# Four split-weight buffers, Fourier tiles by outputs, early swaps of q, and a softmax scaled by GpSimd, in a two-layer encoder

## The chip, the cores and the metric

The kernel runs on one core of a Trainium2 chip. The metric is the device time of one execution in microseconds, the median of several runs. The core has five engines that work side by side, each through its own queue in order: TensorE (PE in the profile; PEld is its weight load), VectorE (DVE), ScalarE (ACT), GpSimd (POOL) and SyncE (SP), which here issues most of the transfers.

## The reference

Two layers of a bidirectional encoder over 272 positions (16 learned meta tokens and 256 tokens), width 2048, in float32:

```python
for i in range(DEPTH):
    h = _rmsnorm(h_stream, norm_mix[i])
    proj = h @ w_in[i]                                  # q | k | v | f | ga | gf
    q = _rope_2d(_rmsnorm(q, q_norm[i]), cos_r, sin_r, cos_c, sin_c)
    k = _rope_2d(_rmsnorm(k, k_norm[i]), cos_r, sin_r, cos_c, sin_c)
    ...
    p = jax.nn.softmax(s, axis=-1)                      # 8 heads on 2 kv heads, head 128
    a_br = attn @ w_attn_br[i]
    fr = jnp.fft.fft2(fg, axes=(1, 3), norm="ortho").real
    s_br = fr.reshape(B, L, FOURIER_WIDTH) @ w_four[i]
    merged = g_attn * a_br + g_four * s_br              # sigmoid gates
    h_stream = h_stream + merged @ w_out[i]
    h2 = _rmsnorm(h_stream, norm_ffn[i])
    up = h2 @ w_up[i]                                   # gate | value, 2 x 5632
    u_gate = _dwconv3_centred(up[..., :D_FF], w_conv[i], b_conv[i])
    h_stream = h_stream + (jax.nn.silu(u_gate) * u_val) @ w_down[i]
return h_stream[:, N_META:]
```

## The kernel before

Activations are kept transposed, channels on the 128 partitions and positions along the free dimension. Each float32 product is made of three matmuls on a type with a shorter mantissa: a high and a low part of the weights (wh, wl) and of the activations (H, L), high times high, high times low and low times high (lines 372 to 374).

All weights run through one stream of 948 chunks of 512 KB, in the order of `order` (lines 191 to 225), with the products of layer 1's last matrices mixed in. A chunk is [128, 4, 256]: four slices of the contracted dimension by 256 outputs. `load_raw` (257) fetches a chunk on SP's queue into one of `RAW = 7` buffers `raw` (in the last feed-forward, every third chunk into one of two buffers `raw5`). `split_w` (294) rounds it on ACT into wh (300) and takes the remainder on DVE into wl (303); `wp` gives wh and wl three buffers each. `advance` (269) loads ahead and puts the splits up to `LOOK = 2` chunks ahead into the list `todo`; `pump` emits them, one after every sixth matmul of a `group` (346). In layer 0 the Fourier weights are folded first: `fold_w` (288) adds and subtracts the halves of a chunk on DVE into the single buffer `wpm` (291), which is then split in place of the raw chunk.

Besides the weight stream, generators in `shadow` are advanced one at a time by `step`, also after every sixth matmul: statistics, rotary work, attention, transposes. `push(gen, wait)` adds one. The order of instructions on each engine is set by a planner that takes the program's order as priority and the costs of a model; inside `manual_schedule` (lines 741, 1168, 1170) and `keep_in_program_order` the order written is the order issued.

The branches of a layer follow `BRANCH_ORDER`. `four_group` (388) multiplies the Fourier branch by its weights, from two chunks. Each of these chunks holds, for two of the four blocks of the contracted dimension and both signs e, all 256 outputs. The loop makes the first 128 outputs (m = 0) from chunk 0 and then chunk 1, and then the other 128 (m = 1) from both again; so both are split (`pump(i0 + 1)`, 395) before it begins. In layer 1 these weights, and those of the Fourier input, have been folded into DRAM beforehand (`prefold`), and the Fourier input is one long product `folded_f` (805) of 16 chunks, placed between the second and the third group of q, with ACT and DVE ordered by hand (1168 to 1172).

For q, `head_evac` (902) brings a group out of PSUM, and a generator `q_stage` (1011) does the rest: `swap` (921) exchanges halves of 64 and 32 channels by four transfers on SP's queue, then the statistics, then `rope` (927) on DVE. The tiles of `head_evac`, `swap`, the gates and the folds share one ring `r` of seven buffers.

`attention` works on 18 items per layer (two kv heads; the meta queries and 4 heads x 2 blocks). For an item, `scores` makes the product, its maximum and the exponentials with their sum (ACT, into the tile pe, 1078); `normalise` (1081) takes the reciprocal of the sum on DVE and writes pe times it into one of three tiles pn, as 256 columns (1086) and three copies of the 16 meta columns (1087); `transposed` (1091), an item later, transposes pn on PE and splits it into PH and PL; `values` multiplies by V.

GpSimd does little: powers for the norms (`pow_half`, 513), and between the branches and the last feed-forward `weight_sums` (553): a tiny copy `tick` that waits for the latest wl, then a DRAM transfer, over and over.

Of the kernel before, what the change touches and what calls it, by code (L numbers as in the profile page):

```python
# [10 lines left out]
F32 = mybir.dt.float32  # L11
# [167 lines left out]
def encoder_kernel(ctx, tc, xT, params, consts, bmat, cfold, csign, w_fl, w_f64c, w_in, w_abr, w_four, w_f64, w_out, w_up, w_down, w_vn, w_dn, w_dt, out):  # L179
# [72 lines left out]
            chunks.append(ch)  # L252
    st = {"raw": 0, "fetch": 0, "next": 0, "grp": 0}
    raws, splits = {}, {}
    RAW, LOOK = 7, 2

    def load_raw(i):
        src, n = chunks[i]
# [22 lines left out]
    def pump(upto=None):  # L281
        if upto is None:
            if todo:
                todo.pop(0)[1]()
        while upto is not None and todo and todo[0][0] <= upto:
            todo.pop(0)[1]()

    def fold_w(i):
# [2 lines left out]
            tc.keep_in_program_order(nc.vector.tensor_tensor(r[:, o:o + 2], raws[i][:, 0:2], raws[i][:, 2:4], op=op))  # L291
        raws[i] = r

    def split_w(i, a, b, parts="hl"):
        if i not in splits:
            splits[i] = tuple(wp.tile([P, CW, MG * P], F32R, tag=t, name=f"{t}{i}") for t in ("wh", "wl"))
        h, lo = splits[i]
        r = raws[i]
        if "h" in parts:
            nc.scalar.copy(h[:, a:b], r[:, a:b])  # L300
        st["wl"] = lo
        if "l" in parts:
            nc.vector.tensor_tensor(lo[:, a:b], r[:, a:b], h[:, a:b].bitcast(F32), op=ALU.subtract)  # L303
            if b == CW:
                del raws[i]
# [82 lines left out]
    def four_group(key, fr, x64, w64, evac):  # L388
        k, chs = order[st["grp"]]
        assert k == key, (k, key)  # L390
        st["grp"] += 1
        i0 = st["next"]
        st["next"] += len(chs)
        advance(i0 + 1 + LOOK)
        pump(i0 + 1)
        ws = [splits.pop(i0 + j) for j in range(2)]
        for m in range(MG):
            sl = slice(m * P, (m + 1) * P)
            ps = [psum.tile([P, 512], F32, tag="mm", name=f"ps_s{m}{e}") for e in range(2)]
            for j in range(2):  # L400
                h, lo = ws[j]
                for c in range(2):
                    kt = 2 * j + c
                    for e in range(2):
                        x = al(fr[:, kt, e])
                        o2 = st2(ps[e][:, :2 * TH].rearrange("p (r n) -> p r n", r=2))
                        nc.tensor.matmul(o2, h[:, 2 * e + c, sl], x, start=kt == 0, stop=False)
                        nc.tensor.matmul(st2(ps[e][:, :TH]), lo[:, 2 * e + c, sl], x[:, 0], start=False, stop=e == 1 and kt == 3)
                    step()
                    pump()  # L410
                if m == 1 and j == 0:
                    advance(i0 + 2 + LOOK)
            nc.tensor.matmul(st2(ps[0][:, :TH]), w64[:, sl], al(x64), start=False, stop=True)
            evac(m, ps)
# [194 lines left out]
    for l in range(DEPTH):  # L609
# [6 lines left out]
        with tc.tile_pool(name=f"mix{l}", bufs=1) as mp:  # L616
# [391 lines left out]
            for pn in pns:  # L1008
                nc.gpsimd.memset(pn[:, 0:P], 0.0)

            def q_stage(i, qp, qsq):
                kv, j = i // 2, i % 2
                sl = slice(2 * j, 2 * j + 2)
                if j == 0:
                    qvs.append(small.tile([P, 9], F32, tag="qv", name="qv"))
                    qsms.append(small.tile([P, 2, 4, NM], F32, tag="sqm", name="sqm", bufs=2))
                qv, qsm = qvs[kv], qsms[kv]
                qs = swap(qp)
                yield 3
                nc.vector.tensor_copy(qsm[:, :, 2 * j:2 * j + 2, :], qsq[:, :, 0:NM].unsqueeze(1).to_broadcast([P, 2, 2, NM]))  # L1020
                d4 = qv[:, 4 * j:4 * j + 4]
# [25 lines left out]
            def attention(kv, rq):  # L1047
# [11 lines left out]
                def scores(item):  # L1059
# [13 lines left out]
                    nc.vector.tensor_reduce(mx, ss[:, :T], axis=AX.X, op=ALU.max)  # L1073
                    nb = small.tile([P, 1], F32, tag="nb", name="nb")
                    nc.vector.tensor_scalar(nb, mx, rcol, -1.0, op0=ALU.mult, op1=ALU.mult)
                    pe = mp.tile([P, T], F32, tag="pe", name="pe", bufs=2)
                    sm = small.tile([P, 1], F32, tag="sm", name="sm")
                    nc.scalar.activation(hv(pe), de(ss[:, :T]), AF.Exp, bias=nb, scale=rcol, accum_out=sm)
                    return pe, sm

                def normalise(pe, sm):
                    rs = small.tile([P, 1], F32, tag="rs", name="rs")
                    nc.vector.reciprocal(rs, sm)
                    pn = pns[cnt[0] % 3]
                    cnt[0] += 1
                    nc.vector.tensor_scalar(pn[:, P:3 * P], pe[:, NM:T], rs, None, op0=ALU.mult)
                    nc.vector.tensor_scalar(pn[:, 0:96].rearrange("p (a b) -> p a b", b=32)[:, :, 0:NM], _rep(pe[:, 0:NM], 3),
                                            rs, None, op0=ALU.mult)
                    return pn

                def transposed(item, pn):
# [59 lines left out]
            for i in range(4):  # L1151
                if not (last and i == 1):
                    ps = group((l, "q", i), xr(lo), W)
                    qq = head_evac(ps, prm[:, P_QN + l:P_QN + l + 1], "qp", lo)
                if last:
                    if i in (0, 2):
                        until(hold, "vt" if i == 0 else "fold")
# [8 lines left out]
                if last and i == 1:  # L1166
                    until(hold, "ahead")
                    with tc.manual_schedule(engines={mybir.EngineType.DVE}):
                        ps = group((l, "q", i), xr(lo), W)
                        with tc.manual_schedule(engines={mybir.EngineType.Activation}):  # L1170
                            qq = head_evac(ps, prm[:, P_QN + l:P_QN + l + 1], "qp", lo)
                            folded_f(slots, E)
                    o1_tiles()
                    push(folded_chan(E), 1)
# [335 lines left out]
def _four(w):  # L1510
# [6 lines left out]
    w64 = np.zeros((d, 64, D), w.dtype)  # L1517
    w64[:, 0:8] = w64[:, 32:40] = w[:, [P * (2 * i + m) + HC for m in range(2) for i in range(4)]]
    w64 = np.ascontiguousarray(w64.reshape(d, 64, NG, MG * P).transpose(0, 2, 1, 3))
    return _tiles(wz[:, rows]), w64  # L1520


def _fl(w):
# [47 lines left out]
```

## Time and profile before

| | |
|---|---|
| median of 3 runs | 2402.76 us (2401.09 to 2405.47) |
| profiled execution | 2399.24 us, of which span 2397.2 us |
| granted TensorE clock | 0.998 |
| DMA, mean | 276 GB/s |

The span is the time from the first to the last instruction; the profiled execution's own time stands beside it. Busy times count an engine's instructions, without waits. In the rows of waits, the engine and line that waited come first, then what ended the wait, then the total, the number and the longest. In a timeline row come start, duration, engine, line, operation, tiles, and in brackets the idle time before it and what ended it.

### The profile page before, as it was taken

The numbers are of one execution on the slowest core, as the hardware profiler recorded it, in microseconds if no ns is written. First come the engines' busy times: TensorE is split into PE (matmuls) and PEld (weight loads), VectorE is DVE, ScalarE is ACT, GpSimd is POOL, SyncE is SP. The second block draws the span as 40 slices with busy tenths as digits, with TensorE's granted clock in tenths as the row PEclk, the third lists the DMA queues.
The fourth block names the chain that finished last, engine by engine and source line by source line (L and its number), as shares of the span: only waits on it lengthen the run. The fifth ranks groups of instructions, "written<-read, shape, count | busy, mean of one in ns | idle before, by whom it ended". The sixth has DMA issues, their size and how long they took to land.

```text
span 2397.2 us, 47622 instructions
## 1 busy us (share of the span) xinstructions
PE 2367.0 (99%) x18992; PEld 2305.8 (96%) x18992; DVE 1819.8 (76%) x2889; ACT 1307.1 (55%) x1893; POOL 133.4 (6%) x265
## 2 busy tenths in 40 slices
PE   9999999999999999999999999999999999999999
PEld 8999999999999999999998999999989999999988
DVE  7787867877767556777568887776878889888798
ACT  6555534554444334444455555445676666666565
POOL 0000100100000000000000000000000000000000
PEclk9999999999999999999999999999999999999999
DMA  7556999989999999999875646888889988988887
GB/s 278 173 159 216 289 295 304 297 278 346 313 303 327 315 330 314 316 327 308 264 256 181 190 150 216 264 291 247 290 294 301 323 291 301 305 304 279 260 279 251
DMA packets 171215, 660.69 MB, mean 276 GB/s; under 512 B 19424, under 2 KB 24672, under 8 KB 170096
## 3 DMA queue, kind: packets, MB, share of 16 engines
q1 hardware_dynamic: 152528, 538.07, 64.0%
q0 software_dynamic: 17024, 117.45, 19.4%
q8 instruction: 149, 2.44, 0.4%
q10 hardware_dynamic: 1440, 2.13, 0.3%
q14 instruction: 74, 0.61, 0.1%
HBM read 635.91 MB, written 136.31 MB: 322 GB/s over the span
## 4 chain that ended last, share of the span: by engine, by line
PE 81%; DVE 6%; ACT 2%; DMA 1%; issue 1%; SPq 0%; POOL 0%; ACTq 0%; DVEq 0%; POOLq 0%
PE ps_p L1415 9%; PE ps_ug L374 6%; PE ps_ug L373 6%; PE ps_ug L372 6%; PE ps_uv L368 4%; PE ps_d L374 3%; PE ps_uv L373 3%; PE ps_uv L372 3%; PE ps_d L373 3%; PE ps_uv L374 3%; PE ps_d L372 3%; DVE wl L303 3%; PE ps_o L372 2%; PE ps_o L373 2%; PE ps_o L374 2%; PE ps_uv L369 2%
## 5 line engine op out<-in xcount | busy, mean ns | idle before, releaser
L303 DVE TENSOR_TENSOR wl<-raw,wh 128x1024 fp32r<-128x1024 f32 (+1 forms) x937 | 1127.6, 1217 | 469.8 <-ACT wh L300 458.4
L300 ACT CAST wh<-raw 128x1024 fp32r<-128x1024 f32 (+1 forms) x937 | 964.6, 1040 | 752.1 <-PE ps_ug L373 197.2
L374 PE MATMUL ps_ug<-xHL,wl 128*128 128x272 f32 (+1 forms) x1408 | 390.6, 277 | 0.8 <-DVE wl L303 0.6
L372 PE MATMUL ps_ug<-xHL,wh 128*128 128x272 f32 (+1 forms) x1408 | 390.7, 278 | 0.0
L373 PE MATMUL ps_ug<-xHL,wh 128*128 128x272 f32 (+1 forms) x1408 | 390.0, 277 | 0.0
L373 PEld LDWEIGHTS ps_ug<-xHL,wh 128*128 128x128 f32 x1408 | 267.4, 190 | 2.1
L372 PEld LDWEIGHTS ps_ug<-xHL,wh 128*128 128x128 f32 x1408 | 267.4, 190 | 2.1
L374 PEld LDWEIGHTS ps_ug<-xHL,wl 128*128 128x128 f32 x1408 | 267.5, 190 | 1.6 <-DVE wl L303 1.5
L372 PE MATMUL ps_uv<-xHL,wh 128*128 128x272 f32 x704 | 196.4, 279 | 0.0
L373 PE MATMUL ps_uv<-xHL,wh 128*128 128x272 f32 x704 | 196.4, 279 | 0.0
L374 PE MATMUL ps_uv<-xHL,wl 128*128 128x272 f32 x704 | 196.4, 279 | 0.0
L372 PE MATMUL ps_d<-gHL,wh 128*128 128x272 f32 x704 | 196.4, 279 | 0.0
L373 PE MATMUL ps_d<-gHL,wh 128*128 128x272 f32 x704 | 196.4, 279 | 0.0
L374 PE MATMUL ps_d<-gHL,wl 128*128 128x272 f32 x704 | 196.4, 279 | 0.0
L1415 PE MATMUL ps_p<-wh,opnd 128*128 128x512 f32 x688 | 177.5, 380 | 0.5 <-ACT wh L300 0.5
L368 PE MATMUL ps_uv<-xHL,wh 128*128 128x512 f32 x448 | 150.8, 383 | 0.1
L372 PE MATMUL ps_ga<-xHL,wh 128*128 128x272 f32 (+1 forms) x512 | 144.0, 281 | 0.0
L372 PE MATMUL ps_gf<-xHL,wh 128*128 128x272 f32 (+1 forms) x512 | 143.0, 279 | 0.0
L374 PE MATMUL ps_gf<-xHL,wl 128*128 128x272 f32 (+1 forms) x512 | 141.8, 277 | 0.0
L373 PE MATMUL ps_ga<-xHL,wh 128*128 128x272 f32 (+1 forms) x512 | 141.8, 277 | 0.0
L374 PE MATMUL ps_ga<-xHL,wl 128*128 128x272 f32 (+1 forms) x512 | 141.8, 277 | 0.0
L373 PE MATMUL ps_gf<-xHL,wh 128*128 128x272 f32 (+1 forms) x512 | 141.8, 277 | 0.0
(372 smaller groups left out, 5840.8 us busy)
## 6 DMA issues: line engine op xcount, KB each, us to landing
raw<-in_w_up SPq DMA_DIRECT2D x320, 512.0 KB, 5.6
raw<-in_w_in SPq DMA_DIRECT2D x191, 512.0 KB, 4.5
raw<-in_w_down SPq DMA_DIRECT2D x88, 512.0 KB, 6.8
raw<-ft SPq DMA_DIRECT2D x80, 512.0 KB, 4.8
raw<-in_w_out SPq DMA_DIRECT2D x64, 512.0 KB, 6.5
ft<-in_w_dn POOLq DMA_DIRECT2D x30, 1024.0 KB, 12.1
raw<-in_w_dn SPq DMA_DIRECT2D x60, 512.0 KB, 5.0
raw<-in_w_abr SPq DMA_DIRECT2D x32, 512.0 KB, 5.6
```

Of the source, the lines that this page charges most:

```text
L300: nc.scalar.copy(h[:, a:b], r[:, a:b])
L303: nc.vector.tensor_tensor(lo[:, a:b], r[:, a:b], h[:, a:b].bitcast(F32), op=ALU.subtract)
L368: nc.tensor.matmul(o2, h[:, c, sl], ab, start=kt == 0, stop=False)
L369: nc.tensor.matmul(o, lo[:, c, sl], ab[:, 0], start=False, stop=kt == nk - 1)
L372: nc.tensor.matmul(o, h[:, c, sl], a, start=kt == 0, stop=False)
L373: nc.tensor.matmul(o, h[:, c, sl], b, start=False, stop=False)
L374: nc.tensor.matmul(o, lo[:, c, sl], a, start=False, stop=kt == nk - 1)
L1415: nc.tensor.matmul(st2(ps[h]), x, al(w[:, 512 * h:512 * h + 512]), start=fresh and (s_, q) in BEGIN and first, stop=(s_, q) in END and end ...
```

## The change

Four edits:

1. `RAW, LOOK = 5, 3`: five raw buffers, splits up to three chunks ahead, and (`split_tiles`) four buffers each for wh and wl. The bytes are the same, 13 tiles before and after.
2. The host lays the Fourier weights out by outputs: a chunk holds both signs and all four blocks of the contracted dimension for 128 outputs. `four_group` then needs chunk m for the outputs m, asks for chunk 0 alone before it starts and for chunk 1 when it comes to m = 1, and calls the second `advance` after the first half instead of after three quarters. The matmuls, their order and widths stay.
3. `swap` is called at once after `head_evac` and its tile handed to `q_stage`, instead of at the first step of `q_stage`; for the second q of layer 1 this is before `folded_f`.
4. In the softmax, the exponentials go straight into the tile pn (the tile pe is gone), the three copies of the meta columns are made by ACT from unscaled values, and GpSimd multiplies the whole tile of 384 columns by the reciprocal in place; DVE keeps the reciprocal.

```diff
-    RAW, LOOK = 7, 2
+    RAW, LOOK = 5, 3
...
+    def split_tiles(i):
+        return tuple(wp.tile([P, CW, MG * P], F32R, tag=t, name=f"{t}{i}", bufs=LOOK + 1) for t in ("wh", "wl"))
+
     def split_w(i, a, b, parts="hl"):
         if i not in splits:
-            splits[i] = tuple(wp.tile([P, CW, MG * P], F32R, tag=t, name=f"{t}{i}") for t in ("wh", "wl"))
+            splits[i] = split_tiles(i)
...
         advance(i0 + 1 + LOOK)
-        pump(i0 + 1)
-        ws = [splits.pop(i0 + j) for j in range(2)]
         for m in range(MG):
             sl = slice(m * P, (m + 1) * P)
             ps = [psum.tile([P, 512], F32, tag="mm", name=f"ps_s{m}{e}") for e in range(2)]
+            pump(i0 + m)
+            h, lo = (w.rearrange("p c n -> p (c n)").rearrange("p (e k n) -> p e k n", e=2, k=4) for w in splits.pop(i0 + m))
             for j in range(2):
-                h, lo = ws[j]
...
-                        nc.tensor.matmul(o2, h[:, 2 * e + c, sl], x, start=kt == 0, stop=False)
-                        nc.tensor.matmul(st2(ps[e][:, :TH]), lo[:, 2 * e + c, sl], x[:, 0], start=False, stop=e == 1 and kt == 3)
+                        nc.tensor.matmul(o2, h[:, e, kt], x, start=kt == 0, stop=False)
+                        nc.tensor.matmul(st2(ps[e][:, :TH]), lo[:, e, kt], x[:, 0], start=False, stop=e == 1 and kt == 3)
                     step()
                     pump()
-                if m == 1 and j == 0:
+                if m == 0 and j == 1:
                     advance(i0 + 2 + LOOK)
...
-            def q_stage(i, qp, qsq):
+            def q_stage(i, qp, qsq, qs):
...
-                qs = swap(qp)
                 yield 3
...
-                    pe = mp.tile([P, T], F32, tag="pe", name="pe", bufs=2)
+                    pn = pns[cnt[0] % 3]
+                    cnt[0] += 1
                     sm = small.tile([P, 1], F32, tag="sm", name="sm")
-                    nc.scalar.activation(hv(pe), de(ss[:, :T]), AF.Exp, bias=nb, scale=rcol, accum_out=sm)
-                    return pe, sm
-
-                def normalise(pe, sm):
+                    nc.scalar.activation(hv(pn[:, P - NM:3 * P]), de(ss[:, :T]), AF.Exp, bias=nb, scale=rcol, accum_out=sm)
+                    nc.scalar.copy(pn[:, 0:96].rearrange("p (a b) -> p a b", b=32)[:, :, 0:NM], _rep(pn[:, P - NM:P], 3))
+                    return pn, sm
+
+                def normalise(pn, sm):
                     rs = small.tile([P, 1], F32, tag="rs", name="rs")
                     nc.vector.reciprocal(rs, sm)
-                    pn = pns[cnt[0] % 3]
-                    cnt[0] += 1
-                    nc.vector.tensor_scalar(pn[:, P:3 * P], pe[:, NM:T], rs, None, op0=ALU.mult)
-                    nc.vector.tensor_scalar(pn[:, 0:96].rearrange("p (a b) -> p a b", b=32)[:, :, 0:NM], _rep(pe[:, 0:NM], 3),
-                                            rs, None, op0=ALU.mult)
+                    nc.gpsimd.tensor_scalar(pn, pn, rs, None, op0=ALU.mult)
                     return pn
...
                     qq = head_evac(ps, prm[:, P_QN + l:P_QN + l + 1], "qp", lo)
+                    qq += (swap(qq[0]),)
...
                             qq = head_evac(ps, prm[:, P_QN + l:P_QN + l + 1], "qp", lo)
+                            qq += (swap(qq[0]),)
                             folded_f(slots, E)
...
-    return _tiles(wz[:, rows]), w64
+    t = _tiles(wz[:, rows]).reshape(d, NG, 2, P, 2, 2, MG, P).transpose(0, 1, 6, 3, 4, 2, 5, 7)
+    return np.ascontiguousarray(t).reshape(d, NG, MG, P, CW, MG * P), w64
```

## The prediction

> **What bounds the kernel now.** The page comes first: the span and the busy times of the engines.
>
> ```profile
> span 2397.2 us, 47622 instructions
> PE 2367.0 (99%) x18992; PEld 2305.8 (96%) x18992; DVE 1819.8 (76%) x2889; ACT 1307.1 (55%) x1893; POOL 133.4 (6%) x265
> ```
>
> TensorE (PE) is busy for 2367.0 of 2397.2 us. The change adds and removes no matmul, so it can only win part of the 30 us in which PE stands still, and a little more where a stall has side effects. The table of busy time by stage tells where those 30 us lie (PE busy is the first engine column, the granted clock stands before the last two).
>
> ```profile
> 120.00:225.00 105.00, 101.24 (x867) 100.14 (x867) 86.97 (x206) 56.66 (x116) 4.29 (x5) 1.00 0.52 172
> 225.00:475.00 250.00, 244.80 (x2091) 242.57 (x2091) 188.54 (x301) 120.50 (x175) 26.47 (x50) 1.00 0.94 297
> 475.00:1243.00 768.00, 768.00 (x6630) 767.92 (x6630) 521.32 (x776) 363.12 (x467) 51.61 (x111) 1.00 0.94 310
> 1243.00:1335.00 92.00, 87.05 (x731) 85.33 (x729) 77.19 (x139) 53.85 (x91) 4.08 (x12) 0.96 0.63 202
> 1335.00:1455.00 120.00, 115.37 (x994) 112.36 (x994) 96.63 (x237) 66.98 (x142) 3.84 (x4) 1.00 0.47 147
> ```
>
> The 768 us of layer 0's feed-forward have no gap, and one matmul there takes 768.0 / 6630 = 0.116 us, so a chunk of 24 matmuls takes 2.8 us. The gaps lie in layer 0's attention (120 to 225), its branches (225 to 475), the folded Fourier product of layer 1 (1243 to 1335) and layer 1's attention (1335 to 1455). Next, PE's waits by cause (total us, times, longest).
>
> ```profile
> PE ps_s L408 <- DVE wl L303: 4.3, 8, 0.7
> PE ps_f L847 <- DVE wl L303: 3.9, 1, 3.9
> PE ps_pt L1095 <- DVE pn L1086: 2.9, 4, 1.3
> PE ps_pv L1119 <- DVE PL L1109: 2.2, 4, 1.2
> PE ps_s L407 <- ACT wh L300: 2.0, 5, 1.1
> PE ps_uv L369 <- DVE wl L303: 1.1, 3, 0.6
> ```
>
> Four of the six rows wait for the split of a weight chunk (wh, wl; `ps_uv` in the last feed-forward), two for the softmax. The change touches both.
>
> **The Fourier branch, `four_group`.** The first group of layer 0 in the order of time, PE and VectorE (DVE):
>
> ```profile
> 222.32 1.28 DVE L291 TENSOR_TENSOR wpm<-raw 128x512 f32<-128x512 f32 x2
> 223.48 0.22 PE L408 MATMUL ps_s<-fr,wl 128*128 128x138 f32 x1
> 224.77 1.23 DVE L303 TENSOR_TENSOR wl<-wpm,wh 128x1024 fp32r<-128x1024 f32 x1 [0.47 <-ACT wh L300]
> 224.79 0.62 PE L407 MATMUL ps_s<-fr,wh 128*128 128x276 f32 x3 [1.09 <-ACT wh L300]
> ```
>
> The group stopped at 223.5, after the eight matmuls (some 0.9 us) of its first chunk: both chunks are needed in turn for the first half of the outputs, and the second was still being folded (L291), rounded (L300) and split (L303). From 223.48 to 224.79 is 1.31 us; 138 columns take 0.06 (half of the 0.116 of 272), so 1.25 are lost, of which the row shows 1.09, since a modelled matmul is longer than its slot. So each of the 13 stalls (8 on L408, 5 on L407) costs some 0.14 more than its row: 4.3 + 2.0 + 13 x 0.14 = 8.1 us. With the tiles by outputs, the second chunk is due only after 16 matmuls and the short one of L413, at about 224.7, and with a fourth split buffer its fold can begin a chunk (2.8 us) earlier. The fold's own buffer stays single, so one chunk's chain, 3.7 us from 222.32 to the end of wl at 226.0, follows the one before it. Even so wl, ready at 226.0, comes 2.8 earlier by 223.2 and is due at 224.7. I take -7.8 (0.3 left); the ends are -3 (fold order unchanged, only the 1.1 us of later need won in each of 8 groups, less than the whole stall) and -8.1. Matmuls, their widths and the bytes are the same, so the new layout itself costs nothing.
>
> **The folded product of layer 1, with the early swap.** Here is the one long stop, on PE, the DMA queue of SyncE (SP) and DVE.
>
> ```profile
> 1292.69 0.33 PE L843 MATMUL ps_f<-hA,wh 128*128 128x276 f32 x1
> 1292.92 0.33 PE L843 MATMUL ps_f<-hA,wh 128*128 128x276 f32 x1
> 1297.73 0.48 PE L847 MATMUL ps_f<-hA,wl 128*128 128x138 f32 x1 [3.89 <-DVE wl L303]
> 1298.45 0.54 PE L843 MATMUL ps_f<-hA,wh 128*128 128x276 f32 x1
> 1298.89 0.53 PE L843 MATMUL ps_f<-hA,wh 128*128 128x276 f32 x1
> 1284.32 0.48 DVE L911 SCALAR_TENSOR_TENSOR qp<-ps_q,prm,rstdB 128x258 f32<-128x258 f32 x1
> 1287.05 2.52 SPq L924 DMA_DIRECT2D qs<-qp  x4
> 1292.93 0.73 DVE L928 TENSOR_TENSOR qs<-qs,cst 128x544 f32<-128x544 f32 x1 [2.54 <-DMA qs<-qp]
> 1296.45 1.22 DVE L303 TENSOR_TENSOR wl<-raw,wh 128x1024 fp32r<-128x1024 f32 x1
> 1310.00:1320.00 10.00, 10.00 (x92) 9.88 (x91) 9.85 (x15) 7.20 (x12) 0.00 (x0) 1.00 0.86 268
> ```
>
> The swap of q's halves stood behind raw loads on SP until 1287.05, DVE waited 2.54 us for it in front of the rotary work, and wl, behind that in a hand-ordered queue, came late: PE stood 3.89 us, with the same 0.14 more 4.05. After the stop a pair of matmuls takes 0.44 us instead of 0.23, and 12 pairs do: 12 x 0.21 = 2.5. (The granted clock of 0.96 over the 92 us of that stage is 3.7 us of missing clock, part of it inside the stop.) Together 6.6 us. Two edits meet here. Issued right after `head_evac` (q is evacuated by 1284.8), the four swap DMAs of 0.6 each are out by 1287.3 and land 3.3 later, at 1290.6: DVE, idle from 1290.4, would start at once. And the fourth buffer puts this wl before the rotary work instead of behind it. What is late next is the wl of the third chunk: 1290.6, plus the 3.5 of rotary work between 1292.93 and 1296.45, plus 1.2 makes 1295.3. PE would reach the second chunk's wl at 1297.73 - 4.05 = 1293.7 and the third's ten pairs (2.3) later, at 1296.0. From there DVE has almost no air (9.85 of 10 us between 1310 and 1320), so part of the stop can come back in slices. I take -6.0; the ends are -6.6 and 0. The raw load that the swap now stands in front of leaves at 1287.3 instead of 1286.6, which its buffers hide.
>
> **Buffers elsewhere: four for splits, five for raw chunks.** Who ends the waits of SP's queue and of ScalarE (ACT):
>
> ```profile
> SPq L264 <- DVE wl L303: 1106.4, 557, 6.2
> ACT wh L300 <- DMA raw<-fv: 2.9, 1, 2.9
> raw<-in_w_up SPq DMA_DIRECT2D x320, 512.0 KB, 5.6
> ```
>
> Loads wait for buffers, not buffers for loads. With five raw buffers a chunk's load starts two chunks (5.6 us) later against its split; five periods are 14 us, less a split of 2.4 (223.60 to 226.0 above) and a landing of 5.6 in the median. Where landings are slow (225 to 1243, DMA share 0.94), some splits will find their data up to 2 us late; behind such a wh on ACT stand evacuations and activations, but the split itself is now a chunk (2.8 us) earlier than PE needs it. I take 0 (ends 0 and +2; nothing in the rows promises a gain). The mixed stream of the last feed-forward is also held by its two raw5 buffers, which stay. There the fourth split buffer should take most of the split waits on `ps_uv` and its neighbours (1.1 of the row above and about as much on other lines): -1.5, ends 0 and -2.2.
>
> **The softmax.** By tile, before: 36 of each.
>
> ```profile
> L1086 DVE TENSOR_SCALAR pn<-pe,rs x36: 343/353/355, 127.8 to 1451.8; 128x256 f32<-128x256 f32 x36
> L1087 DVE TENSOR_SCALAR pn<-pe,rs x36: 243/246/268, 128.0 to 1452.1; 128x48 f32<-128x48 f32 x36
> L1099 ACT CAST PH<-ps_pt x12: 197/218/230, 130.0 to 1420.3; 128x64 fp32r<-128x64 f32 x12
> L493 POOL MEMSET V<- 128x256 f32 x1 | 0.3, 315 | 0.0
> L492 POOL MEMSET ones<- 128x128 f32 x1 | 0.2, 204 | 0.0
> L513 POOL TENSOR_TENSOR rq<-qv,mhalf 128x9 f32<-128x9 f32 x4 | 8.2, 2043 | 107.9 <-DVE qv L1029 107.9
> 226.13 1.27 POOL L558 COPY tick<-wl 128x1 f32<-128x1 f32 x1 [14.26 <-DVE wl L303]
> 226.13 1.23 DVE L303 TENSOR_TENSOR wl<-raw,wh 128x1024 fp32r<-128x1024 f32 x1
> L1083 DVE RECIPROCAL rs<-sm x36: 154/158/166, 127.3 to 1451.6; 128x1 f32<-128x1 f32 x36
> L1095 PE MATMUL ps_pt<-cst,pn x108: 272/273/302, 128.7 to 1455.1; 128*128 128x128 f32 x108
> ```
>
> DVE loses 36 x 0.60 = 21.5 us of work. ACT gains a copy of 48 columns, about 0.21 each by L1099, 7.6 in all, beside the reciprocal. GpSimd (POOL) gains a pass over 384 columns. The trace has no such operation. The two memsets give 0.87 ns per column, so 0.43 us from 128 to 384; that is the low end. The high end is L513's 2.04 us. I take 0.6, nearest to the memsets, plus 0.1 of hand-over, against about 0.7 now (0.35 + 0.25 and a hand-over). But a one-column copy on POOL lasted 1.27 us beside a wl of 1.23 on DVE, so a scaling that starts under a wl can be held for it, and a wl under a scaling likewise. From the end of the reciprocal to the first transpose there are 0.5 to 4.6 us in the 36 items (the first: 127.3 + 0.16 to 128.7; each has three transposes, the last three from 1454.8 on). If every scaling took a given latency, and the transposes kept their places, the shortfalls of all 36 add up to 0.7 us at a latency of 1.0, 2.8 at 1.4, 9.4 at 2.0, 15.6 at 2.4 and 23.9 at 2.8. I reckon with a mean near 1.1, some 1 to 2 us lost. On the other side 0.6 us of DVE less per item lets PL and the reciprocal come sooner, which can give back half of the 2.2 on L1119. Sum 0, ends -4 and +14. On POOL the scalings stand behind the power of L513 (once in each attention, 2 us) and, after 194 us, behind ticks that wait for a wl; a late one of these delays the transposes directly.
>
> The Trainium skill speaks against this edit: "SBUF — State Buffer", section "Who interferes with whom", says that a DVE instruction with two inputs in SBUF and a GpSimd instruction that reads SBUF exclude each other for the whole instruction. The pair of rows at 226.13 agrees. "GPSIMD Engine Reference", section 3.1, gives about 2.6 cycles per element at 1.2 GHz for elementwise work; by that 384 columns would be an estimated 0.83 us, and the sum would be about 1 us worse.
>
> **The sum.** -7.8 - 6.0 - 1.5 + 0 + 0 = -15.3, with 0.3 for the ACT copies -15.0. The profiled execution took 2399.24 us, 2397.2 of it span; it would be 2384.2. It stands 3.5 under the median of the runs, 2402.76, to which the same 15 are applied: 2387.8, said as 2388.
>
> **The rivals.** (1) The lookahead is used up elsewhere: DVE at 98% and the single fold buffer bring half of the long stop and a third of the Fourier stalls back, 3 + 3 us: 2394. The 9.85 speaks for it, DVE's 2.54 us of idling in front of the swap against it. (2) The port: scalings held under wl, mean latency 1.7 to 2, +6 to +9: 2394 to 2397. For it speaks the tick at 226.13; against it, only wl and the rotary work of DVE have two SBUF inputs in this stage. (It is the rule of the Trainium skill, "SBUF — State Buffer", named above, taken at full weight.) (3) Slower than before: the same scaling at 2.8 us (an operation nearer to L513 than to the memsets, plus a wl): +24 - 15 = +9, 2412. It decides from 2.4 us on, where the shortfalls eat the gain. (4) The change does not do what it says: the planner orders DVE so that wl stays behind the rotary work and the fold where it was; 2400 to 2403. (5) Starved by five raw buffers: +2 to +5 on the forecast, 2390 to 2393, inside its range.
>
> **Chances.** The forecast with (5), 2381 to 2393: 0.60. (1): 0.13. (2): 0.12. (4): 0.08. (3): 0.07. A measurement of this kernel tells about 0.2% (4.8 us) from no change, so faster means under 2398: 0.60 + 0.13 + 0.11 = 0.84; same 0.09; slower 0.07. The range takes in (1) and (2): 2381 to 2399.
>
> **What would show it.** Right: no wait rows for `ps_s` in layer 0, a `ps_f` wait under 1 us with the granted clock at 1.00 from 1290 to 1310, DVE's wait for `qs` gone, and transposes that wait no longer in sum than 2.9 us. Wrong: `ps_pt` waiting for POOL's pn by several us, PL waits grown, wh waiting for raw in many places, or a new wl wait inside the folded product.

## The result, and the profile after

The changed kernel takes 2395.68 us (median; 2393.42 to 2396.88), the kernel before, run beside it, 2402.28 us (2399.01 to 2405.47). The ratio is 0.9972, with a 95% interval from 0.9962 to 0.9982: faster by about 6.6 us, where 14.8 were forecast. The profiled executions are 2395.68 us (span 2393.9) after and 2399.24 us (span 2397.2) before.

Both executions issue the same matmuls on the weights, in the same order but for a few in the last feed-forward, so the start of one and the same matmul can be compared in the two traces, and the difference between two such points is what a stage gained or lost (us, changed kernel minus before):

| stage (time in before) | forecast | measured |
|---|---|---|
| start, 0 to 56.5 | 0 | +0.9 |
| layer 0, attention, to 222 | 0 | -0.2 |
| layer 0, branches, to 475 | -7.8 (the Fourier term) | +3.1 |
| layer 0, feed-forward, to 1243 | 0 | 0.0 |
| layer 1, q and folded product, to 1304 | -6.0 | -6.1 |
| layer 1, attention, to 1455 | 0 | 0.0 |
| layer 1, branches, to 1700 | 0 | +5.7 |
| last feed-forward and the rest | -1.5 | -6.6 |

(A forecast of +0.3 for ACT's copies goes with the attention stages.) The folded product came out as forecast and the last feed-forward better. The branches of both layers, where the Fourier products lie, turned from the largest gain into the largest loss. The table of busy time by stage shows the same for PE:

```profile
225.00:475.00 250.00, 239.34 (x2053) 238.10 (x2053) 183.99 (x297) 118.39 (x172) 24.98 (x49) 1.00 0.93 294
...
1243.00:1335.00 92.00, 90.10 (x783) 88.55 (x782) 80.76 (x144) 54.95 (x94) 4.08 (x12) 1.00 0.67 217
...
1455.00:1700.00 245.00, 241.18 (x2142) 240.19 (x2141) 173.29 (x280) 122.72 (x179) 13.00 (x28) 1.00 0.84 261
```

The folded product (1243 to 1335) rose from 87.05 to 90.10 us of PE work, and its granted clock from 0.96 to 1.00. But layer 0's branches fell from 244.80 to 239.34. In layer 1's branches (1455 to 1700) the kernel before has this row, without any gap:

```profile
1455.00:1700.00 245.00, 245.00 (x2189) 245.00 (x2188) 178.04 (x290) 125.92 (x183) 14.57 (x30) 1.00 0.86 270
```

There 3.8 us of gaps are new. PE's waits after, the longest totals first:

```profile
PE ps_a L375 <- DVE se L1208: 6.5, 8, 1.9
PE ps_gf L375 <- DVE se L1208: 6.2, 6, 2.0
PE ps_f L442 <- ACT wh L303: 6.0, 2, 4.4
PE ps_pt L1094 <- POOL pn L1087: 5.1, 5, 1.4
PE ps_ga L375 <- DVE se L1208: 1.9, 2, 1.3
PE ps_pv L1117 <- ACT PH L1107: 1.6, 3, 0.6
PE ps_pv L1118 <- DVE PL L1108: 1.2, 1, 1.2
PE ps_ss L920 <- ACT qps L912: 1.0, 2, 0.8
PE ps_f L845 <- DVE qp L913: 0.9, 1, 0.9
PE ps_ug L377 <- DVE wl L306: 0.6, 1, 0.6
```

The rows on `ps_s` are gone, as forecast: no Fourier product waits for its weights. In their place stand three rows that before does not have, 6.5 + 6.2 + 1.9 = 14.6 us in 16 waits, one behind each of the 16 Fourier products of the two layers. The groups that follow a Fourier product (`ps_a`, `ps_gf`, `ps_ga`, first matmul on L375) wait for `se`, DVE's instruction on line 1208 that takes the Fourier product's PSUM out. So they wait not for weights but for a PSUM bank.

One such place in layer 1, in the timeline of the changed kernel (start, duration, engine, line):

```profile
1473.29 0.22 PE L410 MATMUL ps_s<-fr,wl 128*128 128x138 f32 x1
1473.35 0.27 PE L415 MATMUL ps_s<-x,w 96*128 96x138 f32 x1
...
1473.53 1.05 ACT L303 CAST wh<-raw 128x1024 fp32r<-128x1024 f32 x1 [0.18 <-ACT mH L1229]
...
1474.49 0.26 ACT L1207 COPY se<-ps_s 128x138 f32<-128x138 f32 x1
...
1474.63 1.22 DVE L306 TENSOR_TENSOR wl<-raw,wh 128x1024 fp32r<-128x1024 f32 x1
1474.65 0.28 ACT L1207 COPY so<-ps_s 128x138 f32<-128x138 f32 x1
...
1475.30 0.27 PE L415 MATMUL ps_s<-x,w 96*128 96x138 f32 x1
...
1475.76 0.30 DVE L1208 TENSOR_TENSOR se<-ps_s,se 128x138 f32<-128x138 f32 x1
...
1476.11 0.38 PE L375 MATMUL ps_gf<-xHL,wh 128*128 128x258 f32 x1 [0.54 <-DVE se L1208]
```

The first half of the outputs (m = 0) is finished by the short matmul of L415 at 1473.35. Its evacuation could start at about 1473.6. But the last matmul on the chunk's weights was the one before it (L410), and with the tiles by outputs that chunk is used by no later matmul. So its wh and wl buffers came free about 0.1 us ahead of the PSUM, and the split of a later chunk went into them first: ACT's cast of 1.05 us at 1473.53 stands ahead of the copies of `se` and `so`, and DVE's remainder of 1.22 us at 1474.63 ahead of its two additions. The order on each engine was fixed before the run, by the planner from its model's times; the trace shows the order that came out. It is the same everywhere: behind all 16 Fourier products of the changed kernel a cast stands ahead of the two copies of m = 0, in the kernel before behind none. PE has finished m = 1 by about 1475.5, and it waits until 1476.1 for the banks of m = 0.

In layer 0 the same happens with two remainders in front (226.83, in the timeline of the same trace), and the wait is 2.03 us:

```profile
226.83 2.58 DVE L306 TENSOR_TENSOR wl<-raw,wh 128x1024 fp32r<-128x1024 f32 x2 [1.18 <-ACT wh L303]
...
229.34 0.29 DVE L1208 TENSOR_TENSOR se<-ps_s,se 128x138 f32<-128x138 f32 x1
...
229.69 0.38 PE L375 MATMUL ps_gf<-xHL,wh 128*128 128x272 f32 x1 [2.03 <-DVE se L1208]
```

In the kernel before, the first chunk was still needed for the first matmuls of m = 1, so its buffer came free a quarter of the product later, when the evacuation of m = 0 was under way. The same place there, m = 0 finished at 1475.32 and nothing ahead of ACT's copy:

```profile
1475.32 0.27 PE L413 MATMUL ps_s<-x,w 96*128 96x138 f32 x1
...
1475.52 0.28 ACT L1206 COPY so<-ps_s 128x138 f32<-128x138 f32 x1 [0.19 <-PE ps_s L408]
...
1475.69 0.28 ACT L1206 COPY se<-ps_s 128x138 f32<-128x138 f32 x1
...
1476.53 1.05 ACT L300 CAST wh<-raw 128x1024 fp32r<-128x1024 f32 x1 [0.56 <-ACT se L1206]
```

### The profile page after: what moved, and what is told of

It reads as the page before. It is cut to its first block, busy times and chain, and to the rows that moved or that the text cites. A ratio compares the mean times of both kernels' runs of the same rounds, so it can differ in the third digit from the quotient of the medians.

```text
span 2393.9 us, 47708 instructions
## 1 busy us (share of the span) xinstructions
PE 2359.2 (99%) x18992; PEld 2304.8 (96%) x18992; DVE 1801.8 (75%) x2817; ACT 1312.1 (55%) x1929; POOL 190.6 (8%) x301
## 5 line engine op out<-in xcount | busy, mean ns | idle before, releaser
L375 PE MATMUL ps_ug<-xHL,wh 128*128 128x272 f32 (+1 forms) x1408 | 390.8, 278 | 0.0
L375 PEld LDWEIGHTS ps_ug<-xHL,wh 128*128 128x128 f32 x1408 | 267.4, 190 | 2.1
L375 PE MATMUL ps_uv<-xHL,wh 128*128 128x272 f32 x704 | 196.4, 279 | 0.0
L375 PE MATMUL ps_d<-gHL,wh 128*128 128x272 f32 x704 | 196.4, 279 | 0.0
L560 POOL COPY tick<-wl 128x1 f32<-128x1 f32 x112 | 37.2, 332 | 1516.4 <-DVE wl L306 1516.4
L375 PE MATMUL ps_gf<-xHL,wh 128*128 128x272 f32 (+1 forms) x512 | 143.3, 280 | 6.2 <-DVE se L1208 6.2
L375 PE MATMUL ps_ga<-xHL,wh 128*128 128x272 f32 (+1 forms) x512 | 144.1, 281 | 1.9 <-DVE se L1208 1.9
```

Of the source, the lines that this page charges most:

```text
L375: nc.tensor.matmul(o, h[:, c, sl], a, start=kt == 0, stop=False)
L560: tc.keep_in_program_order(nc.gpsimd.tensor_copy(tick, st["wl"][:, 0, 0:1].bitcast(F32)))
```

## The experiments

The theory from the traces: the layout by outputs brings the waits, since it frees a buffer just ahead of the PSUM of the same matmuls, and in the planner's order what comes free first is filled first. The main rival: the fourth split buffer brings them, since more splits stand in the list ahead of an evacuation. A second question is whether the place of the call in the program has a part. Each kernel was timed beside the kernel before (medians there 2400.2 to 2401.2 us, for the change 2402.28); the last two columns come from its profile. The ratio is not exactly the quotient of the two medians: for e2 it stands for 15.1 us (12.0 to 18.0), where the medians differ by 13.0. A difference of one or two us between rows says nothing.

| kernel | median, us | ratio to before (95%) | waits on `se`/`so`, us | layer 0 / layer 1 branches, us |
|---|---|---|---|---|
| the change | 2395.68 | 0.9972 (0.9962 to 0.9982) | 14.6 | +3.1 / +5.7 |
| e1_layout_only | 2411.01 | 1.0037 (1.0024 to 1.0051) | 12.7 | +4.5 / +5.8 |
| e2_lookahead_only | 2387.73 | 0.9937 (0.9925 to 0.9950) | 1.9 | -4.2 / 0.0 |
| e6_old_tiles | 2381.45 | 0.9921 (0.9907 to 0.9935) | 3.6 | -2.8 / 0.0 |
| e3_w64_first | 2392.25 | 0.9959 (0.9946 to 0.9971) | 8.9 | +2.6 / +4.3 |
| e5_feed_behind | 2395.30 | 0.9980 (0.9971 to 0.9989) | 13.9 | +5.7 / +5.7 |
| e7_both | 2393.50 | 0.9970 (0.9958 to 0.9981) | 9.7 | +1.6 / +4.3 |
| e9_high_last | 2381.81 | 0.9926 (0.9913 to 0.9940) | 1.7 | -5.1 / +0.9 |
| e13_high_last_alone | 2382.60 | 0.9926 (0.9913 to 0.9938) | 1.8 | -5.4 / +0.4 |

**e1_layout_only: the layout without the rest.** Before, with edit 2 of the change alone:

```diff
-        pump(i0 + 1)
...
+            pump(i0 + m)
...
-                        nc.tensor.matmul(o2, h[:, 2 * e + c, sl], x, start=kt == 0, stop=False)
+                        nc.tensor.matmul(o2, h[:, e, kt], x, start=kt == 0, stop=False)
...
-                if m == 1 and j == 0:
+                if m == 0 and j == 1:
```

> Before, with the Fourier weight tiles by outputs and nothing else (three split buffers, seven raw ones, late swaps, scaling by DVE). First theory (layout): a chunk's buffer comes free one short matmul ahead of its group's PSUM, so the split copies of a later chunk go ahead of the evacuation, and the next group waits for PSUM: 0.5 to 1 us behind each of layer 1's 8 s groups and 1 to 2 us behind layer 0's, 12 to 20 us of such waits by rows on `se`, which replace the stalls inside the groups: 2400 to 2409 us. Rival (the fourth split buffer brings the waits, whatever the layout): no waits on `se` behind the s groups, the stalls of 8 us gone or halved: 2394 to 2398 us.

Measured 2411.01 us, slower than before by 0.24 to 0.51%. Its waits:

```profile
PE ps_gf L372 <- DVE se L1206: 5.4, 6, 1.6
PE ps_a L372 <- DVE se L1206: 5.2, 8, 0.9
...
PE ps_ga L372 <- DVE se L1206: 2.1, 2, 1.6
PE ps_s L407 <- DVE wl L303: 2.1, 5, 0.9
```

With three split buffers the same 16 waits are there (12.7 us), and layer 1's branches lose 5.8 us (5.7 in the changed kernel). The theory holds, though the time is 2 us above the range that it gave.

**e2_lookahead_only: the buffers without the rest.**

```diff
-    RAW, LOOK = 7, 2
+    RAW, LOOK = 5, 3
...
-            splits[i] = tuple(wp.tile([P, CW, MG * P], F32R, tag=t, name=f"{t}{i}") for t in ("wh", "wl"))
+            splits[i] = tuple(wp.tile([P, CW, MG * P], F32R, tag=t, name=f"{t}{i}", bufs=LOOK + 1) for t in ("wh", "wl"))
```

> Before, with four split and five raw buffers and nothing else (Fourier tiles by inputs as before). First theory (layout): no waits on `se` behind the s groups, the splits come early enough that the stalls inside the groups shrink, and the last feed-forward gains its 6 us as in the changed kernel: 2388 to 2393 us. Rival (the fourth buffer brings the waits): rows of 10 us and more on `se`, about 2398 to 2401 us.

Measured 2387.73 us, 13.0 us under before and just below the first theory's range: one of the four edits gives twice what all four give together. Of its waits:

```profile
PE ps_f L843 <- DVE qp L911: 3.3, 1, 3.3
...
PE ps_gf L372 <- DVE so L1207: 1.5, 3, 0.7
PE ps_ss L918 <- ACT qps L910: 1.0, 2, 0.8
PE ps_s L407 <- DVE th L1226: 0.7, 2, 0.4
```

Nothing on `se`, 1.9 us on `so`, and no Fourier product waits for weights any more. The rival falls, but for a small part: the 1.9 us all lie in layer 0, where in seven of the eight products a remainder that starts after the short matmul now stands ahead of DVE's additions (before, in none).

**e6_old_tiles: the change without the layout.** The changed kernel with `four_group` and the host's order of before (the diff of e1 backwards).

> The changed kernel with the Fourier weight tiles by inputs again (the other three parts stay). First theory (layout): no wait above 1 us in all on `se` behind the s groups; the 13.0 us of the lookahead alone, and the stop at the folded product shorter by 2 to 3 us more through the early swap, softmax 0 to -3 us: 2380 to 2386 us. Rival (the three parts don't add up, DVE or GpSimd takes back what the lookahead gave): 2388 us or more.

Measured 2381.45 us, within the theory's range: the layout costs the changed kernel 14.2 us by the medians, 12 by the ratios. `se` is gone from the list; `so` stays with 3.6 us, all in layer 0. The rows give no cause for its growth from e2's 1.9, and it was not followed up.

**e3, e5, e7: is it the short matmul, or the place of the call?** e3 puts the short matmul ahead of the last four; e5 leaves it and puts the second call for splits behind the evacuation; e7 does both.

```diff
+                    if kt == 3:
+                        nc.tensor.matmul(st2(ps[0][:, :TH]), w64[:, sl], al(x64), start=False, stop=False)
...
-                        nc.tensor.matmul(st2(ps[e][:, :TH]), lo[:, e, kt], x[:, 0], start=False, stop=e == 1 and kt == 3)
+                        nc.tensor.matmul(st2(ps[e][:, :TH]), lo[:, e, kt], x[:, 0], start=False, stop=kt == 3)
...
-            nc.tensor.matmul(st2(ps[0][:, :TH]), w64[:, sl], al(x64), start=False, stop=True)
```

```diff
-                if m == 0 and j == 1:
-                    advance(i0 + 2 + LOOK)
             nc.tensor.matmul(st2(ps[0][:, :TH]), w64[:, sl], al(x64), start=False, stop=True)
             evac(m, ps)
+            if m == 0:
+                advance(i0 + 2 + LOOK)
```

> The changed kernel, with the short 64-row matmul of an s group moved ahead of the group's last four matmuls, so that buffer and PSUM are finished by the same matmuls. First theory, in its narrow form (the one matmul between them decides who goes first): waits on `se` fall from 14.6 us to under 5 us, 2384 to 2389 us. If they fall by less than 3 us, the order of the two is set by something else than that matmul, and the time stays at 2394 to 2397 us.

> The changed kernel, with the second call for splits of an s group put behind the first evacuation (in the program; the short matmul stays last). If the place in the program decides who goes first on DVE and ACT: waits on `se` and `so` fall from 14.6 us to under 4 us, 2382 to 2387 us. If the moment at which the buffer comes free decides (the copies are taken as soon as they can run, wherever they are called): waits stay above 10 us, 2393 to 2397 us.

> The changed kernel with both: the short matmul ahead of the group's last four, and the second call for splits behind the first evacuation. Layout theory: buffer and PSUM are free at the same moment and the evacuation is called first, so the waits behind s groups go (under 3 us of 14.6): 2381 to 2386 us. If the waits stay above 6 us, a tie is not broken by the place in the program: 2390 to 2395 us.

e5 changes nothing that can be measured (13.9 us of waits, 2395.30 us): the place of the call in the program is not what sets the order. e3 and e7 both missed their ranges for the theory: the waits fall only to 8.9 and 9.7 us. e7 lies in the range of its second reading, that the place in the program breaks no tie, but there was no tie. The rows tell why; those of e3:

```profile
PE ps_a L375 <- DVE so L1209: 3.6, 8, 0.9
PE ps_gf L375 <- DVE so L1209: 3.1, 5, 0.9
...
PE ps_ga L375 <- DVE so L1209: 1.1, 2, 0.7
```

Now it is `so`, the other sign's bank, that PE waits for. In e3 the bank of `se` is complete early, but the last matmul of all is the low one (L410) of `so`'s bank, and the last on wh is the high one just ahead of it. The buffer of wh still comes free one short matmul before that bank, and the split slips in between the two copies: in e3's trace a cast stands between them in all 16 products.

**e9 and e13: the bank complete no later than the buffer.** In the last step of the contracted dimension the low matmul goes ahead of the high one as well, so that the last matmul both frees wh and completes the bank. e9 has this with the later call of e5, e13 without it.

```diff
+                    if kt == 3:
+                        nc.tensor.matmul(st2(ps[0][:, :TH]), w64[:, sl], al(x64), start=False, stop=False)
...
-                        nc.tensor.matmul(o2, h[:, e, kt], x, start=kt == 0, stop=False)
-                        nc.tensor.matmul(st2(ps[e][:, :TH]), lo[:, e, kt], x[:, 0], start=False, stop=e == 1 and kt == 3)
+                        if kt == 3:
+                            nc.tensor.matmul(st2(ps[e][:, :TH]), lo[:, e, kt], x[:, 0], start=False, stop=False)
+                        nc.tensor.matmul(o2, h[:, e, kt], x, start=kt == 0, stop=kt == 3)
+                        if kt < 3:
+                            nc.tensor.matmul(st2(ps[e][:, :TH]), lo[:, e, kt], x[:, 0], start=False, stop=False)
...
-            nc.tensor.matmul(st2(ps[0][:, :TH]), w64[:, sl], al(x64), start=False, stop=True)
```

> The changed kernel with the short matmul and the last low-weight matmuls ahead of the last high-weight ones, and the second call for splits behind the first evacuation: PSUM is now complete no later than the high-weight buffer is free. If what comes free first is taken first (the layout theory, by moments): waits behind s groups on `se` and `so`, 14.6 us in the changed kernel, under 4 us, 2381 to 2386 us. If the waits stay above 6 us, neither the moment nor the place in the program sets who goes first, and what does stays open: 2390 to 2395 us.

> As e9_high_last, but the second call for splits stands where the change put it, ahead of the evacuation. If the moment at which buffer and PSUM come free is all that decides: no waits to speak of behind s groups, as in e9_high_last, 2380 to 2385 us. If the moment only makes a tie, which the place in the program then breaks: the copies go first again, waits on `se` and `so` of 5 us or more, 2388 to 2394 us.

2381.81 and 2382.60 us, not to be told apart. Three kinds of matmuls put in another order within the last step, with nothing else touched (e13), give 13 us by the medians, 11 by the ratios. The timeline of e13 at the same place, the short matmul of m = 0 at 1463.92:

```profile
1463.92 0.27 PE L407 MATMUL ps_s<-x,w 96*128 96x138 f32 x1
...
1464.52 0.28 ACT L1211 COPY se<-ps_s 128x138 f32<-128x138 f32 x1
...
1464.75 0.28 ACT L1211 COPY so<-ps_s 128x138 f32<-128x138 f32 x1
...
1464.92 1.05 ACT L303 CAST wh<-raw 128x1024 fp32r<-128x1024 f32 x1
...
1465.66 0.30 DVE L1212 TENSOR_TENSOR se<-ps_s,se 128x138 f32<-128x138 f32 x1
```

The copies now stand ahead of the cast, DVE's addition starts 1.74 us after the short matmul (2.41 in the changed kernel), and PE has no wait there, nor behind any other Fourier product of layer 1. The 1.8 us that are left lie in layer 0.

**The other terms one by one.** The swap alone (e11), five raw buffers alone (e10), the softmax alone (e4):

```diff
-                qs = swap(qp)
...
                     qq = head_evac(ps, prm[:, P_QN + l:P_QN + l + 1], "qp", lo)
+                    qq += (swap(qq[0]),)
...
```

```diff
-    RAW, LOOK = 7, 2
+    RAW, LOOK = 5, 2
```

```diff
-                    pe = mp.tile([P, T], F32, tag="pe", name="pe", bufs=2)
+                    pn = pns[cnt[0] % 3]
...
-                    nc.vector.tensor_scalar(pn[:, P:3 * P], pe[:, NM:T], rs, None, op0=ALU.mult)
...
+                    nc.gpsimd.tensor_scalar(pn, pn, rs, None, op0=ALU.mult)
```

> Before with the swap of each q chunk right behind its evacuation, and nothing else. The forecast's term: the stop of 6.6 us at the folded product falls to about 1 us and the slow clock behind it goes, 6.0 us less: 2393 to 2396 us. Rival (the weights' splits end almost as late as the swap, so that PE waits for `wl` instead): 2 to 4 us of stop stay, 2397 to 2400 us.

> Before with five raw buffers instead of seven and nothing else (three split buffers). The forecast put two raw buffers fewer at nothing: 2399 to 2403 us. Rival (starved raw buffers, the forecast's fifth rival, hidden in the other runs behind the gain of the fourth split buffer): 2405 us or more, with waits on `raw` or longer ones on `wh`.

> Before, with the exponentials written to the padded tile, copied by ACT and scaled in place by GpSimd, and nothing else. First theory (the softmax part is neutral, as in the forecast): 2400 to 2404 us, waits on `ps_pt` no more than 1.5 us from those of before. Rival (GpSimd held by DVE's splits costs time that the other parts hide in the changed kernel): 2405 to 2412 us, with the longer waits on `pn`.

e11: 2397.59 us, 0.9989 (0.9980 to 0.9999), less than the forecast's gain and in the range of the rival. Its profile, taken of the fastest of its 11 runs, speaks more for the forecast: the stage gives 5.5 us, while the layer 1 attention and the last feed-forward give back 0.5 and 0.6. Of the rival a wait for wl stays, shorter than its 2 to 4 us:

```profile
PE ps_f L847 <- DVE wl L303: 1.4, 2, 1.3
```

e10: 2402.16 us, 1.0001 (0.9992 to 1.0011): no difference that can be measured. e4: 2397.99 us, 0.9986 (0.9978 to 0.9995), a small gain, outside the range of the first theory on the good side. In its profile the two attentions give 0.5 us together, and the q and folded stage 2.5; how a lighter DVE shortens that stop was not followed up, nor was a gain of 1.1 in layer 0's branches.

**e8_look_swap and e14_high_last_dve: do the terms add up?** e8 is before with the buffers and the swap (the diffs of e2 and e11). e14 is e9 with the softmax of before (the diff of e4 backwards).

> Before with four split and five raw buffers and the early swap; tiles by inputs, scaling by DVE. The forecast's terms for these two parts: the stop at the folded product falls from 6.6 us to about 1 us at clock 1.00 (3.3 us with the buffers alone); the buffers give what they gave alone, 13.0 us, so 2384 to 2387 us. Rival (the stop is set by DVE's and ACT's splits, not by the swap): wait on `qp` 3 us or more, 2387 to 2389 us.

> As e9_high_last, but with the softmax scaled by DVE from pe as before. The softmax part alone gave -0.14% of before (about -3 us); if that is its own, this takes 2383 to 2387 us; if it came from the order that the planner happened to find, this is within 1 us of e9_high_last's 2381.8, on either side; if GpSimd's scaling costs time that the rest hides, below 2380 us.

e8: 2383.63 us, 0.9930 (0.9918 to 0.9943), just below its range. The wait at the folded product is 1.2 us on `qp`, against 3.3 in e2. The two edits alone (0.9937 and 0.9989) would make 0.9926 together, so within the intervals they add up. e14: 2383.79 us, 0.9930 (0.9916 to 0.9943); this interval and e9's (0.9913 to 0.9940) overlap widely, so no gain or loss of the softmax can be shown there.

**e12_three_raw: how far the trade of buffers goes.** e6 with `RAW, LOOK = 3, 4`, a fifth split buffer for two raw ones.

> The changed kernel with tiles by inputs, three raw buffers and a fifth split buffer. If the fourth buffer already took what lookahead can give: 2380 to 2383 us, as with five and four. If the shortage of splits still binds somewhere: below 2379 us. If three raw buffers no longer cover a load's time: 2386 us or more, with longer waits on `wh` or `wl`.

2600.71 us, 1.0839 (1.0822 to 1.0856). Of its waits:

```profile
ACT wh L303 <- DMA raw<-in_w_up: 265.1, 149, 8.4
ACT wh L303 <- DMA raw<-in_w_down: 121.0, 62, 7.7
```

ACT waits for raw chunks all over the kernel, for `in_w_up` alone 265.1 us. With three raw buffers the rival of starved loads, which costs nothing at five, takes over the whole kernel. The fifth split buffer came in the same run, so what it does alone is not shown.

## Why the prediction was right or wrong

The stages of four kernels beside the forecast, by the same matmul in each trace (us against before):

| stage | forecast | the change | e2 (buffers) | e6 (without layout) | e13 (order mended) |
|---|---|---|---|---|---|
| layer 0, branches | -7.8 | +3.1 | -4.2 | -2.8 | -5.4 |
| layer 1, branches | 0 | +5.7 | 0.0 | 0.0 | +0.4 |
| q and folded product | -6.0 | -6.1 | -2.1 | -6.1 | -6.1 |
| last feed-forward | -1.5 | -6.6 | -7.2 | -7.7 | -6.9 |
| whole span | -15.0 | -3.3 | -13.6 | -15.9 | -17.8 |

**The Fourier term: wrong, and this is the step that failed.** "Matmuls, their widths and the bytes are the same, so the new layout itself costs nothing." It looked at when a chunk is needed and not at when its buffer is given back. The layout moved that from three quarters of a product to its half, just ahead of the PSUM of the first half, and 16 waits of up to 2.0 us came, half of them in layer 1, where there had been no stall to remove. The removal of the stalls itself worked: in e13, where the waits are nearly gone, layer 0's branches gain 5.4 us of the 7.8; 1.8 us of the rest are waits on `se`. That the layout is needed for it is not shown: with the tiles by inputs e2 and e6 gain 4.2 and 2.8 us there, and the whole kernels (e6 and e13) come out alike. None of the rivals had this mechanism. That the measured time lies near rival (1)'s 2394 and within rival (2)'s 2394 to 2397 is chance: rival (1) let half of the long stop and a third of the Fourier stalls return, and neither did; rival (2) laid the loss on the softmax, and the attention stages lost nothing. Of the signs of being right three came true (no rows on `ps_s` for weights, the short stop in the folded product at full clock, no wait for `qs`), the fourth did not (transposes wait 5.1 us, not 2.9 at most); none of the signs looked behind the Fourier product.

**The folded product: right.** The stop is 0.9 us (`qp` L913), the granted clock 1.00, the stage 6.1 us shorter. What is late next is not the third chunk's wl, as the prediction had it, but DVE's evacuation of q, which frees a PSUM bank. The runs show the two edits that meet there: the buffers alone leave a wait of 3.3, the swap alone one of 1.3, both together about 1.

**The last feed-forward: right in its cause, mis-sized.** -1.5 with the far end at -2.2, measured -6.6, and -6.0 to -7.7 in the nine other kernels with four split and five raw buffers. The forecast added up rows of waits (2.2 us in all). In these traces a matmul of 258 columns is drawn 0.28 us long, while the next one starts 0.11 us after it; so stalls under about 0.3 us leave no row, and longer ones lose some 0.17 each. By the starts of the matmuls before there are a dozen stalls above 0.2 us behind 1740, some 5 us together, and smaller ones of some 3; after there is one of 0.7. The prediction had made this correction for the Fourier stalls (0.14 each) but not here.

**The raw buffers at nothing: right** (e10, within -0.08 and +0.11%). ACT did wait longer for chunks, as foreseen (for `in_w_up` 2.2 us in 2 waits before, 13.0 in 7 in the changed kernel), but PE's only wait in the two feed-forwards after is the one of 0.6 us on `ps_ug`.

**The softmax at nothing: right in the sum, wrong in its size.** GpSimd's scaling was taken as 0.6 us; the rows of the tile pn after (minimum, median and maximum in ns):

```profile
L1081 ACT COPY pn<-pn x36: 216/231/240, 126.8 to 1449.7; 128x48 f32<-128x48 f32 x36
L1087 POOL TENSOR_SCALAR pn<-pn,rs x36: 1234/1246/2137, 128.0 to 1450.1; 128x384 f32<-128x384 f32 x36
```

It takes 1.24 us undisturbed, twice the value taken. From the end of the reciprocal to the scaled tile it is 2.05 us on average over the 36 items, and over 2.8 us in 11 of them. In ten of these 11 the same thing happens, and the prediction missed it: ACT's new copy stands behind the cast of a weight chunk (1.03 us), and that cast also releases the split on DVE, so the scaling becomes ready 0.25 us after the split has begun and is held by it (rows in the last section). Such an item takes 3.1 us instead of some 1.44. By the prediction's own table of shortfalls a latency of 2.0 costs 9.4 us. That is the premise of rival (2), and it came true; its price did not. The waits on `ps_pt` grew by 2.2 us (2.9 to 5.1), those of `ps_pv` for PL shrank by 1.0 (2.2 to 1.2), and the attention stages are -0.2 and 0.0 us. The table held only "if the transposes kept their places", and they did not: the smallest gap between scaled tile and transpose is 0.06 us, and items with a late tile mostly have later transposes, with other matmuls put ahead of them: on average the first transpose starts 3.06 us after the reciprocal, 2.43 before.

**The sum.** Against the forecast's -15.0 the Fourier term is 16.6 worse (+3.1 and +5.7 for -7.8), the last feed-forward 5.1 better, the start 0.9 worse (its first loads landed later in this execution), the rest within 0.6: -3.3 in the span. The medians differ by 6.6, since the profiled execution of before lies 3 us under its own median.

## What to carry to other kernels

When a layout or a loop order changes, write down for each buffer not only when its content is needed but when its last reader ends, and what the list of waiting work will put there at that moment; a buffer that comes free just ahead of a PSUM bank lets the planner put a 1 us cast ahead of a 0.3 us evacuation that PE needs. Order the last matmuls of a group so that the bank is complete no later than the weights are released. And run a bundle's edits one by one: here, by the medians, the buffer edit alone gave 13 us, all four 6.6, and three of the four 19.

## What was not expected of the hardware

GpSimd's operation of 384 columns in place took 1.24 us alone. The Trainium skill, "GPSIMD Engine Reference", section 3.1, gives about 2.6 cycles per element at 1.2 GHz, measured there on an addition of two tensors of 2048 elements; by that 384 columns would be an estimated 0.83 us. The operation here has one tensor input and is shorter, and the measurement decides.

A scaling that starts under a split of DVE is held for nearly all of the split (timeline of the changed kernel):

```profile
129.31 1.03 ACT L303 CAST wh<-raw 128x1024 fp32r<-128x1024 f32 x1
...
130.24 0.23 ACT L1081 COPY pn<-pn 128x48 f32<-128x48 f32 x1
...
130.37 1.23 DVE L306 TENSOR_TENSOR wl<-raw,wh 128x1024 fp32r<-128x1024 f32 x1 [0.77 <-ACT wh L303]
...
130.62 2.08 POOL L1087 TENSOR_SCALAR pn<-pn,rs 128x384 f32<-128x384 f32 x1 [1.39 <-ACT pn L1081]
```

It ends 1.10 us after the split's end, so only some 0.14 of its 1.24 us lay beside the split. So it goes in all 11 items whose scaling starts under a split. That agrees with the Trainium skill, "SBUF — State Buffer", section "Who interferes with whom". The other way round the records show no such hold:

```profile
140.03 1.24 POOL L1087 TENSOR_SCALAR pn<-pn,rs 128x384 f32<-128x384 f32 x1 [2.61 <-PE ps_s L1072]
...
140.62 1.22 DVE L306 TENSOR_TENSOR wl<-raw,wh 128x1024 fp32r<-128x1024 f32 x1
```

The split starts 0.59 us into the scaling and neither takes longer; the same holds for all seven splits that start 0.48 to 1.22 us into an otherwise undisturbed scaling, and no split in that trace is longer than 1.23 us. One operation of the rotary work, also with two inputs in SBUF, starts only 0.05 us after a scaling has begun, and then it is the scaling that grows, to 1.79 us:

```profile
1379.05 1.79 POOL L1087 TENSOR_SCALAR pn<-pn,rs 128x384 f32<-128x384 f32 x1 [2.10 <-DVE rs L1086]
...
1379.10 0.72 DVE L932 TENSOR_TENSOR qp<-qp,qs 128x544 f32<-128x544 f32 x1
```

GpSimd's spans are rough in the profile, so when the scaling has read all its columns, and which of the two really came first at 1379.05, stays open.
